# Seven block products for eight in half of an attention output projection, and smaller steps at the layer ends

## The chip, the cores and the metric

The kernel runs on one core of one Trainium2 chip. The metric is the device time in microseconds of one execution. The numbers below come from three timed runs and from one profiled execution of the kernel before.

## The reference

A decoder trunk of two layers works on 256 positions of width 2048, in float32. Layer 0 mixes by recurrences (RG-LRU and HGRN2), layer 1 by dilated attention with 16 heads of 128. Each is followed by an output projection, a residual sum, a norm and a squared-ReLU MLP of width 8192. What the change touches:

```python
out = (num / den).reshape(bsz, seq, D_MODEL).astype(h.dtype)   # the 16 heads, side by side
return out @ w_o                                               # 256 x 2048 by 2048 x 2048
...
h = h + mix
h = h + squared_relu_mlp(rms_norm(h, norm_mlp[layer]), w1[layer], w2[layer])
...
return rms_norm(h, final_norm)
```

## The kernel before

**Weights.** All weights come as units of 128 x 2048 numbers (1 MB). A unit is read into a `raw` tile (three buffers) and split in two: ACT casts the high part `hi` (`L104`), DVE subtracts to get the low part `lo` (`L105`), three buffers each. One float32 product is then three matmuls on PE: activation high by weight high, high by low, and low by high. `unit()` takes the next unit in a fixed list, `units`, and has the unit two places further fetched and split, with a raised priority (`stream`).

**Activations.** `bufa` holds the normed input of a projection, feature by feature, each feature block with its high and low half (512 numbers). `bufb` holds what goes into an output projection: block k of `bufb` is head k of the attention. `xres` (tile `xall` in the profile) is the residual, token by token: two halves j of 128 tokens, four column groups n of 512.

**A plain projection to tokens** (`tokens`, `out_project`): for a column group n, four units g (four feature blocks each) are multiplied for both token halves j, 2 x 4 x 3 = 24 matmuls of 512 columns a unit, into two banks of PSUM. `add_res` adds them to `xres`, and `to_features` transposes the four blocks back to `bufa` (two halves, each run from a list `turns` between units) and, for n < 2, forms the sums below.

**Seven products for eight** (`blocks`): for a pair of column groups and the first half of the features, the product is a 2 x 2 block product (token halves by even and odd feature blocks, even and odd rows of the weight by the two column groups) in the manner of Strassen and Winograd. Seven block products of twelve matmuls each replace eight: `a`, `t1`, `t2`, `c`, `t3`, `d`, `t4`. `t1`, `t2`, `t3` and `c` take sums of activation blocks, which `combos` and `part_forms` put into `formx` or `formh`. `t1`, `t2`, `t3` and `t4` take sums of weight units, which `combine` makes: tile `t` and tile `s`, by DVE (`L132`) or by an accumulating transfer on POOL's queue (`L144` to `L150`). The other half of the features goes through four plain units `n` (24 matmuls each). `ORDERS` fixes the sequence of the eleven units; the banks are `alpha`, `delta`, `gamma` (pool `p`) and `beta` (`pd`, `po` or `pt`). The MLPs (`first`, `second`) and the values of the attention already work so; the two output projections `w_out` and `w_o` are plain. In `second` a DVE sum makes the weight of `t4` (`s` plus `d`); in `first` and in the values a transfer does.

**What sets the order around the change.** A scheduler orders the instructions of every engine by priority and data; `mm` and `turn` chain the large products and the transposes of residuals on PE in the order of the program, whatever else is ready. The tiles of PSUM are allotted in the order of the program: whoever asks for `pd` or `po` waits until the earlier holder has been read.

**The attention's last heads.** For each head, `scores` makes q and k (two units), turns them (`rope`, on DVE), multiplies (`pl`), forms the softmax (DVE and ACT), transposes it (`pd`) and copies it (`pT`); `mix` multiplies it with the values (`po`) and splits the result into `bufb`. After head 15, `out_project(w_o, ...)` follows.

**Layer ends.** In the last quarter of an MLP, `done` follows each column group: `to_features` in layer 0; in layer 1, `xres` is multiplied by the final gain (`L799`).

Of the kernel before, what the change touches and what calls it, by code (L numbers as in the profile page):

```python
# [10 lines left out]
F32 = mybir.dt.float32  # L11
# [5 lines left out]
OP = mybir.AluOpType  # L17
# [3 lines left out]
P = 128  # L21
S = 256
# [19 lines left out]
def trunk_kernel(ctx, tc, x, xtok, cols, tab, masks, pos, fin, w_in, w_gate, w_out, w_qkv, w_o, w1, w2, out):  # L42
# [22 lines left out]
    units = []  # L65
    made = {}

    def plan(src, n):
        units.extend((src, i) for i in range(n))

    def plan2(src, i):
        for what, u in ORDERS[src is not w1]:
            units.append((src, None if u is None else i + u, what, i))

    where = {"x": (w_in, lambda i: i, 1), "y": (w_in, lambda i: 8 + i, 1), "g": (w_gate, lambda i: i, 1),
# [5 lines left out]
    for layer in range(2):  # L81
        if layer:
            for v, heads in ((0, 24), (32, 8)):
                plan2(w_qkv, v)
                units.extend((w_qkv, v + 8 + i) for i in range(heads))
            plan(w_o, 16)
        for q in range(4):
            for src in (w1, w2):
                for n in range(0, 4, 2):
                    plan2(src, layer * 64 + q * 16 + 4 * n)  # L90
# [35 lines left out]
    def combine(u, src, i, what, i0):  # L126
        def load(name, j, home=wraw):
            held[name] = home.tile([P, 2048], F32, name="raw" if home is wraw else name)
            nc.sync.dma_start(held[name], src[j])

        def add(to, x, y):
            V.tensor_tensor(held[to], held[x], held[y], OP.add)  # L132

        if what == "a":
            load("t1", i0 + 4, both)
            load("a", i)
            held["s"] = both.tile([P, 2048], F32, name="s")
            add("s", "a", "t1")
        elif what in ("n", "d"):
            load(what, i)  # L140
        ahead = units[u + 1][2:3] if u + 1 < len(units) else ()
        if ahead == ("t2",):
            load("c", i0 + 5)
            nc.gpsimd.dma_start(held["t1"], src[i0 + 5], accum_op=OP.add)  # L144
            add("s", "s", "c")
        if ahead == ("t4",) and src not in T4_DMA(w1, w2, w_qkv):
            add("s", "s", "d")
        made[u] = Weights(held[{"t1": "s", "t2": "s", "t3": "t1", "t4": "s"}.get(what, what)])
        if what == "c" and src in T4_DMA(w1, w2, w_qkv):
            nc.gpsimd.dma_start(held["s"], src[i0 + 1], accum_op=OP.add)  # L150

    def fetch_first():
# [178 lines left out]
            V.scalar_tensor_tensor(r, t, 1.5, r, op0=OP.add, op1=OP.mult)  # L331

    def tokens(src, i0, mov, kgs=(0, 1, 2, 3), by_k=False):
        ks = range(KB)
        ps = [pmm.tile([P, 512], F32, name="p") for _ in range(2)]
        for g in kgs:
            w = unit(src, i0 + g)
            order = [(j, i) for i in range(4) for j in range(2)] if by_k else \
                [(j, i) for j in range(2) for i in range(4)]
            for j, i in order:  # L340
                k = ks[4 * g + i]
                h, l = w.part(i * 512, 512)
                xh = mov[:, k, j * P:j * P + P]
                xl = mov[:, k, S + j * P:S + j * P + P]
                first, last = g == kgs[0] and i == 0, g == kgs[-1] and i == 3
                mm(ps[j], xh, h, start=first, stop=False)
                mm(ps[j], xh, l, start=False, stop=False)
                mm(ps[j], xl, h, start=False, stop=last)
            turn_some(1)
        return ps  # L350
# [268 lines left out]
    def to_features(n, gname, forms=None):  # L619
        def work(half):  # L620
            k = 4 * n + 2 * half
            with urgent():
                p = psc.tile([P, 2, S], F32, name="pl", bufs=2)
                for j in range(2):
                    for i in range(2):
                        turn(p[:, i, j * P:j * P + P], xres[:, j, (k + i) * P:(k + i) * P + P])
                if forms is None:
                    for i in range(2):
                        split_to(bufa[:, k + i], p[:, i], col(gname, k + i))
                    return  # L630
                z = pair.tile([P, 2, 2, P], F32, name="y4" if half else "y21")
                for i in range(2):
                    A.activation(z[:, i], p[:, i].rearrange("p (j c) -> p j c", j=2), AF.Copy, scale=col(gname, k + i))
                split_to(bufa[:, k:k + 2], z.rearrange("p i j c -> p i (j c)"))
                a11, a21, a12, a22 = (z[:, i, j] for i in range(2) for j in range(2))
                combos(a22, a11, a21, a12, a11, a21, a12, a22)
                part_forms(forms, k // 2, 1, slice(0, 4), z.rearrange("p i j (one c) -> p one (i j) c", one=1))
        turns.extend([0, lambda half=half: work(half)] for half in range(2))

    def out_project(src, gname, kgs):  # L640
        nrm = Norm()
        for n in range(4):
            add_res(tokens(src, 4 * n, bufb, kgs), n, nrm)
            to_features(n, gname, formx if n < 2 else None)
        return nrm
# [3 lines left out]
    def blocks(src, i0, n0, mov, forms, events, final):  # L649
# [4 lines left out]
                "c": lambda i: form(2, i)}  # L654
        alpha, delta, gamma = (pmm.tile([P, 512], F32, name="p") for _ in range(3))
        beta = psc.tile([P, 512], F32, name="pt" if src is w_qkv and i0 else "po" if n0 else "pd", bufs=1)
        bank = {"a": beta, "t1": alpha, "t2": beta, "c": alpha, "t3": beta, "d": gamma, "t4": beta}
        sums = {(0, 0): gamma, (0, 1): beta, (1, 0): alpha, (1, 1): delta}
        opened = []

# [6 lines left out]
                mm(bank, xh, l, start=False, stop=False, skip_group_check=True)  # L667
                mm(bank, xl, h, start=False, stop=i == 3, skip_group_check=True)

        plains = [0, 0]  # L670
        for what, u in ORDERS[src is not w1]:
            w = unit(src, None if u is None else i0 + 4 * n0 + u)
            due = len(later)
            if what != "n":
                times(bank[what], w, side[what])
                if what in events:
                    events[what](bank[what])
            else:
                n, g = divmod(u, 4)
                plains[n] += 1  # L680
                for j in (1, 0) if n else (0, 1):
                    times(sums[n, j], w, lambda i, j=j, g=g: plain(j, 4 * g + i))
                    if plains[n] == 2:
                        final(n, j, sums[n, j])
                flush(due)
            turn_some()
# [60 lines left out]
        blocks(w1, i0, n0, bufa, formx, {"a": hold("y1", A.copy, 2), "t1": hold("y4", V.tensor_copy), "t2": hold("y2", A.copy),  # L747
                                             "t3": u3}, final)

    def second(i0, n0, nrm, r2, r2n, done, gains):  # L750
        def to_x(bank, j, n, r, last):
            at = slice(n * 512, n * 512 + 512)
            with urgent():
                V.scalar_tensor_tensor(xres[:, j, at], bank, r[:, j:j + 1], xres[:, j, at], op0=OP.mult, op1=OP.add)  # L754
                if nrm and last:
                    nrm.add(j, n)

        def u2(bank):
            to_x(bank, 0, n0 + 1, r2n, False)
            if gains:  # L760
                gains()

        def u3(bank):
            to_x(bank, 1, n0 + 1, r2n, True)
            done(n0 + 1)

        blocks(w2, i0, n0, bufb, formh,
               {"a": lambda b: to_x(b, 0, n0, r2, False), "t1": lambda b: to_x(b, 1, n0 + 1, r2, False),
                "t2": u2, "t3": u3},
               lambda n, j, b: to_x(b, j, n0 + n, r2, (n, j) != (1, 1)))  # L770
        done(n0)

    def mlp(layer, nrm, nxt, gname):
# [13 lines left out]
        for q in range(4):  # L787
            ends = nxt if q == 3 else None

            def done(n):  # L790
                if ends is None:
                    return
                if gname:
                    to_features(n, gname, formx if n < 2 else None)
                elif n != LAST:
                    at = slice(n * 512, n * 512 + 512)
                    with urgent():
                        for j in range(2):
                            V.tensor_tensor(xres[:, j, at], xres[:, j, at], fing[n], OP.mult)  # L799

            for n in (0, 2):
                first(layer * 64 + q * 16, n)
# [129 lines left out]
    vg = values(32)  # L932
    for i, bank in enumerate((("po", 1), ("pd", 1), ("pl", 2), ("pl", 2))):
        mix(8 + i, pend[i], vg, *bank)
    for i in range(4):
        mix(12 + i, scores(40 + 2 * i), vg)

    mixers.close()
    pair, formh = open_pairs(1)
    nrm = out_project(w_o, "nmlp1", (0, 1, 2, 3))  # L940
    fnorm = Norm()
    fing = mlp(1, nrm, fnorm, None)
    done = [n for n in range(4) if n != LAST]
# [46 lines left out]
_A = (("a", 0), ("t1", 4))  # L990
_B = (("t2", 5), ("c", None))
_C = (("t3", None), ("d", 1), ("n", 2), ("t4", None), ("n", 3))
ORDERS = (_A + (("n", 6),) + _B + (("n", 7),) + _C, _A + (("n", 7),) + _B + (("n", 6),) + _C)
T4_DMA = lambda w1, w2, w_qkv: (w1, w_qkv)
NOSYNC = mybir.DependencyInfo(mybir.DependencyClass.NoSync, mybir.DependencyReason.DATA)


# [29 lines left out]
def _layout(a):  # L1027
# [25 lines left out]
    def gate(w):  # L1053
# [16 lines left out]
        "pos": c(n(a["positions"]).reshape(1, S)),  # L1070
        "fin": c(n(a["final_norm"]).reshape(1, D)),
        "w_in": c(np.concatenate(w_in)), "w_gate": c(w_gate), "w_out": c(toks(n(a["rec_w_out"][0]))),
        "w_qkv": c(np.concatenate(w_qkv)), "w_o": c(toks(n(a["attn_w_o"][0]))),
        "w1": w1, "w2": w2,
    }

# [17 lines left out]
```

## Time and profile before

| | us |
|---|---|
| three timed runs: median | 2164.65 |
| lowest, highest | 2163.99, 2165.69 |
| the profiled execution | 2164.17 |
| its span, first to last instruction | 2162.0 |
| PE busy in it | 2142.9 |
| DVE busy in it | 1819.7 |
| ACT busy in it | 1268.8 |

The profile shows one execution. Engines: PE multiplies (PEld loads its weights), DVE and ACT work on vectors, POOL and SP only issue transfers here. `L105` is line 105 of the kernel; in a group, `lo<-raw,hi` is the tile that is written and those that are read. A busy time counts each instruction from its start to its end; matmuls overlap, so their busy times add up to more than the time they take.

### The profile page before, as it was taken

What the parts mean: (1) busy time and instruction counts of PE and PEld (TensorE: products, weight loads), DVE (VectorE), ACT (ScalarE), POOL (GpSimd) and SP (SyncE); (2) the same over time, 40 slices, a digit from 0 to 9 for tenths busy, and PEclk for the clock granted to TensorE, in tenths of its full rate; (3) what the DMA queues carried; (4) which work ended last, traced back from release to release, by engine and by line L of the source; (5) the groups of instructions that cost most, each with busy time, mean ns of one, the idle gap of its engine ahead of it and who ended that gap; (6) DMA issues with size and microseconds to landing.
All of it is one profiled execution on the core that took longest, in us unless ns stands there. A gap on an engine that the chain in (4) does not pass through costs nothing.

```text
span 2162.0 us, 27706 instructions
## 1 busy us (share of the span) xinstructions
PE 2142.9 (99%) x11020; PEld 1829.1 (85%) x11020; DVE 1819.7 (84%) x2114; ACT 1268.8 (59%) x1415; POOL 48.0 (2%) x61
## 2 busy tenths in 40 slices
PE   9999999999999999999999999999999999999997
PEld 8999998888888888888788888888888888888886
DVE  7776787689889889889998897767998998998897
ACT  7444485566466566557665545455655755755764
POOL 0000000000000000000000000000000000000000
PEclk9999999999999999999999999999999999999999
DMA  8444446587777777787675556456868777777873
GB/s 319 157 156 162 152 155 214 178 243 246 229 237 250 233 238 243 237 251 226 209 249 197 173 163 227 157 190 218 246 219 254 238 229 246 241 234 228 261 238 129
DMA packets 66432, 468.86 MB, mean 217 GB/s; under 512 B 7408, under 2 KB 8176, under 8 KB 10368
## 3 DMA queue, kind: packets, MB, share of 16 engines
q1 hardware_dynamic: 58176, 410.89, 53.1%
q0 software_dynamic: 7840, 55.61, 13.8%
q8 instruction: 86, 1.41, 0.3%
q10 hardware_dynamic: 288, 0.61, 0.1%
q14 instruction: 42, 0.34, 0.0%
HBM read 464.98 MB, written 2.10 MB: 216 GB/s over the span
## 4 chain that ended last, share of the span: by engine, by line
PE 94%; DVE 3%; ACT 1%; DMA 1%; issue 1%; SPq 0%; DVEq 0%; ACTq 0%
PE p L183 65%; PE pd L183 12%; PE po L183 12%; PE pl L186 2%; DVE lo L105 1%; PE pl L479 1%; PE pt L183 1%; ACT hi L104 1%; DMA raw<-in_w 0%; DMA xall<-in_x 0%; PE pl L863 0%; PE po L884 0%; DVE xall L754 0%; PE pd L876 0%; PE pd L463 0%
## 5 line engine op out<-in xcount | busy, mean ns | idle before, releaser
L104 ACT CAST hi<-raw 128x2048 fp32r<-128x2048 f32 (+2 forms) x468 | 684.0, 1484 | 556.2 <-PE p L183 342.6
L105 DVE TENSOR_TENSOR lo<-raw,hi 128x2048 fp32r<-128x2048 f32 (+2 forms) x468 | 816.5, 1759 | 192.2 <-ACT hi L104 176.4
L183 PE MATMUL p<-hi,bufb 128*128 128x512 f32 x1408 | 450.1, 391 | 3.3 <-DVE xall L754 2.7
L183 PE MATMUL p<-hi,bufa 128*128 128x512 f32 x1136 | 365.8, 391 | 1.0 <-ACT hi L104 0.7
L183 PE MATMUL p<-bufa,hi 128*128 128x256 f32 (+1 forms) x1792 | 365.3, 317 | 0.1
L183 PEld LDWEIGHTS p<-hi,bufb 128*128 128x128 f32 x1408 | 264.1, 188 | 62.2 <-DVE xall L754 6.2
L183 PEld LDWEIGHTS p<-bufa,hi 128*128 128x128 f32 x1792 | 294.2, 190 | 18.6 <-DVE hz L421 0.3
L183 PE MATMUL p<-lo,bufb 128*128 128x512 f32 x704 | 274.4, 390 | 0.9 <-DVE lo L105 0.9
L183 PE MATMUL p<-bufa,lo 128*128 128x256 f32 x1152 | 256.6, 287 | 0.0
L183 PEld LDWEIGHTS p<-hi,bufa 128*128 128x128 f32 x1136 | 213.2, 188 | 48.3 <-DVE y L718 2.4
L105 DVE TENSOR_TENSOR lo<-s,hi 128x2048 fp32r<-128x2048 f32 x102 | 233.2, 2286 | 19.0 <-ACT hi L104 17.0
L104 ACT CAST hi<-s 128x2048 fp32r<-128x2048 f32 x102 | 195.2, 1914 | 52.9 <-PE po L183 22.4
L183 PE MATMUL p<-lo,bufa 128*128 128x512 f32 x568 | 221.9, 391 | 1.9 <-DVE lo L105 1.9
L183 PEld LDWEIGHTS p<-bufa,lo 128*128 128x128 f32 x1152 | 189.7, 191 | 2.7
L183 PEld LDWEIGHTS p<-lo,bufb 128*128 128x128 f32 x704 | 132.2, 188 | 28.0 <-DVE lo L105 1.2
L183 PEld LDWEIGHTS p<-lo,bufa 128*128 128x128 f32 x568 | 106.7, 188 | 25.5 <-DVE lo L105 4.1
L132 DVE TENSOR_TENSOR s<-s,raw 128x2048 f32<-128x2048 f32 x50 | 114.2, 2283 | 3.7 <-DMA raw<-in_w 3.7
L183 PE MATMUL pd<-hi,bufa 128*128 128x512 f32 x288 | 95.2, 392 | 0.0
L183 PE MATMUL p<-hi,formx 128*128 128x512 f32 x288 | 94.9, 390 | 0.0
L105 DVE TENSOR_TENSOR lo<-t,hi 128x2048 fp32r<-128x2048 f32 x34 | 77.8, 2288 | 13.0 <-ACT hi L104 13.0
L183 PE MATMUL po<-hi,bufa 128*128 128x512 f32 x256 | 84.8, 392 | 0.0
L183 PE MATMUL p<-hi,formh 128*128 128x512 f32 x256 | 84.0, 389 | 0.0
(302 smaller groups left out, 2875.8 us busy)
## 6 DMA issues: line engine op xcount, KB each, us to landing
raw<-in_w SPq DMA_DIRECT2D x224, 1024.0 KB, 5.0
raw<-in_w_in SPq DMA_DIRECT2D x46, 1024.0 KB, 4.9
raw<-in_w_qkv SPq DMA_DIRECT2D x46, 1024.0 KB, 4.9
t<-in_w SPq DMA_DIRECT2D x32, 1024.0 KB, 5.6
t<-in_w POOLq DMA_DIRECT2D x32, 1024.0 KB, 8.9
raw<-in_w_out SPq DMA_DIRECT2D x16, 1024.0 KB, 4.9
s<-in_w POOLq DMA_DIRECT2D x16, 1024.0 KB, 9.1
raw<-in_w_o SPq DMA_DIRECT2D x16, 1024.0 KB, 4.9
```

Of the source, the lines that this page charges most:

```text
L104: A.copy(h, w)
L105: V.tensor_tensor(l, w, h.bitcast(F32), OP.subtract)
L132: V.tensor_tensor(held[to], held[x], held[y], OP.add)
L183: chain[:] = [after(T.matmul(*args, **kw), chain)]
L186: chain[:] = [after(T.transpose(out_, in_, ident), chain)]
L479: T.matmul(pl[:, j], kq[:, js], halves(qp[:, js], c, True), start=True, stop=True)
```

## The change

It has five parts.

1. The first pair of column groups of `w_o` goes through `second`, with `src=w_o`, scale 1.0, and an order of its own: a plain unit first (`n`, 6), then `a`, `t1`, `n` 7, `t2`, `c`, `t3`, `d`, `n` 2, `t4`, `n` 3. `t1` gets a bank of its own (`po`), and unit 6 and 7 share `alpha` and `delta` from the start, so that one eviction (`e5`) serves two column groups and `final(1, 0)` comes after `c`. The second pair stays plain.
2. `mixed_forms` makes the sums of activations for it from heads 0 to 7 in `bufb`, in four steps by the last four heads.
3. The weight of `t4` is made by an accumulating transfer everywhere, in `second` too.
4. `to_features` with `forms` starts its second half one unit later than its first.
5. The gain products of column groups 0 and 1 at the end go through `turns`, some units later, without raised priority.

```diff
+    order_of = lambda src: ORDERS[0 if src is w1 else 2 if src is w_o else 1]
...
-            plan(w_o, 16)
+            plan2(w_o, 0)
+            units.extend((w_o, 8 + i) for i in range(8))
...
-        if ahead == ("t4",) and src not in T4_DMA(w1, w2, w_qkv):
-            add("s", "s", "d")
         made[u] = Weights(held[{"t1": "s", "t2": "s", "t3": "t1", "t4": "s"}.get(what, what)])
-        if what == "c" and src in T4_DMA(w1, w2, w_qkv):
+        if what == "c":
             nc.gpsimd.dma_start(held["s"], src[i0 + 1], accum_op=OP.add)
...
-        ks = range(KB)
+        ks = PAIRED if src is w_o else range(KB)
...
-        turns.extend([0, lambda half=half: work(half)] for half in range(2))
+        turns.extend([-half if forms else 0, lambda half=half: work(half)] for half in range(2))
-    def out_project(src, gname, kgs):
-        nrm = Norm()
-        for n in range(4):
+    def out_project(src, gname, kgs, ns=range(4), nrm=None):
+        nrm = nrm or Norm()
+        for n in ns:
...
-        bank = {"a": beta, "t1": alpha, "t2": beta, "c": alpha, "t3": beta, "d": gamma, "t4": beta}
+        bank = {"a": beta, "t1": psc.tile([P, 512], F32, name="po", bufs=1) if src is w_o else alpha, "t2": beta, "c": alpha, "t3": beta, "d": gamma, "t4": beta}
...
+                elif what == "c" and plains[1] == 2:
+                    final(1, 0, alpha)
...
-                    if plains[n] == 2:
+                    if plains[n] == 2 and (n, j, "c" in done) != (1, 0, False):
                         final(n, j, sums[n, j])
...
+        def e5(bank):
+            to_x(bank, 1, n0 + 1, r2, False)
+            if src is w_o:
+                to_x(bank, 0, n0 + 1, r2, False)
...
-                    at = slice(n * 512, n * 512 + 512)
-                    with urgent():
+                    def gain(n=n, at=slice(n * 512, n * 512 + 512)):
                         for j in range(2):
                             V.tensor_tensor(xres[:, j, at], xres[:, j, at], fing[n], OP.mult)
+                    if n < 2:
+                        turns.append([-3, gain])
+                    else:
+                        with urgent():
+                            gain()
...
+    z = both.tile([P, 2048], F32, name="s").rearrange("p (m i j c) -> p m i j c", m=4, i=2, j=2)
+
+    def mixed_forms(m):
+        zm, b = z[:, m], bufb[:, 2 * m:2 * m + 2].bitcast(F32)
+        V.tensor_tensor(zm.rearrange("p i j c -> p i (j c)"), b[..., :S], b[..., S:], OP.add)
+        a11, a21, a12, a22 = (zm[:, i, j] for i in range(2) for j in range(2))
+        combos(a22, a11, a21, a12, a11, a21, a12, a22)
+        part_forms(formx, m, 1, slice(0, 4), zm.rearrange("p i j (one c) -> p one (i j) c", one=1))
+
     for i in range(4):
         mix(12 + i, scores(40 + 2 * i), vg)
+        mixed_forms(i)
...
-    nrm = out_project(w_o, "nmlp1", (0, 1, 2, 3))
+    nrm = Norm()
+    second(0, 0, nrm, 1.0, -1.0, lambda n: to_features(n, "nmlp1", formx), src=w_o, forms=formx)
+    out_project(w_o, "nmlp1", (0, 1, 2, 3), (2, 3), nrm)
...
 _A = (("a", 0), ("t1", 4))
 _B = (("t2", 5), ("c", None))
 _C = (("t3", None), ("d", 1), ("n", 2), ("t4", None), ("n", 3))
-ORDERS = (_A + (("n", 6),) + _B + (("n", 7),) + _C, _A + (("n", 7),) + _B + (("n", 6),) + _C)
-T4_DMA = lambda w1, w2, w_qkv: (w1, w_qkv)
+ORDERS = (_A + (("n", 6),) + _B + (("n", 7),) + _C, _A + (("n", 7),) + _B + (("n", 6),) + _C,
+          (("n", 6),) + _A + (("n", 7),) + _B + _C)
```

The rows of `w_o` are laid out on the host in the paired order of feature blocks (0, 2, 4, 6, 1, 3, 5, 7, then 8 to 15), as those of the MLPs are; `ks = PAIRED` in `tokens` follows it.

More of the change, by code (lines that the diff above doesn't have):

```diff
@@ L66, in trunk_kernel @@
     made = {}
-    def plan(src, n):
-        units.extend((src, i) for i in range(n))
+    order_of = lambda src: ORDERS[0 if src is w1 else 2 if src is w_o else 1]
     def plan2(src, i):
-        for what, u in ORDERS[src is not w1]:
+        for what, u in order_of(src):
             units.append((src, None if u is None else i + u, what, i))
@@ L668, in times @@
                 mm(bank, xl, h, start=False, stop=i == 3, skip_group_check=True)
-        plains = [0, 0]
-        for what, u in ORDERS[src is not w1]:
+        plains, done = [0, 0], []
+        for what, u in order_of(src):
             w = unit(src, None if u is None else i0 + 4 * n0 + u)
             due = len(later)
+            done.append(what)
             if what != "n":
@@ L748, in first, with second @@
                                              "t3": u3}, final)
-    def second(i0, n0, nrm, r2, r2n, done, gains):
+    def second(i0, n0, nrm, r2, r2n, done, gains=None, src=w2, forms=None):
         def to_x(bank, j, n, r, last):
@@ L753, in to_x @@
             with urgent():
-                V.scalar_tensor_tensor(xres[:, j, at], bank, r[:, j:j + 1], xres[:, j, at], op0=OP.mult, op1=OP.add)
+                V.scalar_tensor_tensor(xres[:, j, at], bank, r if isinstance(r, float) else r[:, j:j + 1],
+                                       xres[:, j, at], op0=OP.mult, op1=OP.add)
                 if nrm and last:
                     nrm.add(j, n)
+        def e5(bank):
+            to_x(bank, 1, n0 + 1, r2, False)
+            if src is w_o:
+                to_x(bank, 0, n0 + 1, r2, False)
         def u2(bank):
@@ L765, in u3 @@
             done(n0 + 1)
-        blocks(w2, i0, n0, bufb, formh,
-               {"a": lambda b: to_x(b, 0, n0, r2, False), "t1": lambda b: to_x(b, 1, n0 + 1, r2, False),
-                "t2": u2, "t3": u3},
+        blocks(src, i0, n0, bufb, forms or formh,
+               {"a": lambda b: to_x(b, 0, n0, r2, False), "t1": e5, "t2": u2, "t3": u3},
                lambda n, j, b: to_x(b, j, n0 + n, r2, (n, j) != (1, 1)))
@@ L1072, in _layout @@
         "w_in": c(np.concatenate(w_in)), "w_gate": c(w_gate), "w_out": c(toks(n(a["rec_w_out"][0]))),
-        "w_qkv": c(np.concatenate(w_qkv)), "w_o": c(toks(n(a["attn_w_o"][0]))),
+        "w_qkv": c(np.concatenate(w_qkv)), "w_o": c(toks(n(a["attn_w_o"][0]), PAIRED)),
         "w1": w1, "w2": w2,
```

## Prediction

> **What bounds the kernel now.** I read the page first (span, busy shares, clock), then who waited for whom on PE, then the chain of waits around the projection, then the timelines of DVE and ACT there, then busy times by stage.
>
> ```profile
> span 2162.0 us, 27706 instructions
> PE 2142.9 (99%) x11020; PEld 1829.1 (85%) x11020; DVE 1819.7 (84%) x2114; ACT 1268.8 (59%) x1415; POOL 48.0 (2%) x61
> ```
> ```profile
> PE p L183 <- DVE lo L105: 2.8, 5, 0.9
> PE p L183 <- DVE xall L754: 2.7, 2, 1.4
> ```
> TensorE is the bound, nearly without a hole: all waits of PE together are under 10 us. So a removed matmul is worth its whole spacing, and a hole in PE costs its whole length.
>
> ```profile
> 1394.13 0.11 PE pd L876
> ...
> 1396.32 0.22 PE pl L862 x2
> 1396.54 0.43 PE pl L863 x2
> 1396.97 2.52 PE p L183 x11
> 1399.49 0.43 PE po L884 x2
> ...
> 1403.82 0.11 PE pd L876
> ...
> 1407.15 0.43 PE po L884 x2
> 1407.59 0.24 PE po L885 x2
> ...
> 1408.27 9.46 PE p L183 x39
> 1417.72 0.87 PE pl L186 x8
> 1418.60 21.78 PE p L183 x96
> ```
> This chain is in order of time. Two things are to be seen. First, 96 matmuls take 21.78 us: one costs 0.227 us of PE, not the 391 ns of its own row, since they overlap. Second, the attention of heads 14 and 15 (scores `pl`, transposes of the weights `pd`, mix `po`) lies between products of `w_o` (`p L183`): heads 0 to 11 are enough for three of the first column group's four units, so PE has about 90 products to do while DVE and ACT make the last softmaxes. The stage runs from 1386.5 to 1434.9 (end of column group 1; 1418.60 plus 72 x 0.227): **48.4 us**.
>
> **The change, part by part.** Building the changed program gives the order of instructions on each engine; every time below is from the trace of before.
>
> *The products.* Fifteen block products of twelve matmuls stand for sixteen: 12 x 0.227 = **-2.7 us**. No other matmul goes.
>
> *What covers the softmax.* This decides. The new order starts with unit n6 (24 products, 5.4 us), and then `a` writes bank `pd` and `t1` bank `po`, the banks that heads 14 and 15 still need. The order on PE is therefore: 24 products; `pd` of 14; `po` of 14; `pl` of 15; `pd` of 15; `po` of 15; `a`. Between them stands no product at all. The durations:
>
> ```profile
> 1397.01 0.56 DVE L865 SCALAR_TENSOR_TENSOR as<-pl,tab__181 128x384 f32<-128x384 f32 x1 [1.43 <-PE pl L863]
> 1397.60 0.61 DVE L869 TENSOR_REDUCE nm<-as 128x1 f32<-128x128 f32 x2
> 1398.94 0.17 DVE L871 RECIPROCAL ll<-ll 128x2 f32<-128x2 f32 x1 [0.73 <-ACT as L214]
> 1399.14 0.55 DVE L873 TENSOR_SCALAR as<-as,ll 128x128 f32<-128x128 f32 x2
> ```
> ```profile
> 1398.93 1.28 ACT L214 ACT_TABLE_LOAD   x1
> 1400.22 0.20 ACT L214 ACTIVATE spare<-epsc 128x1 f32<-128x1 f32 x1
> ```
> From the scores' first matmul (1396.15 in PE's timeline) to the end of the scaling (1399.69) are 3.55 us; the transposes take 0.33, the copy of `pT` ends 0.8 after the last one starts (1394.42 to 1395.21), the mix takes 0.65. I step through the new order:
> - The products of `w_o` start at 1386.5 as before; n6 ends at 1391.9.
> - `pl` of 14 now stands behind 15 of the 16 `lo` matmuls of its neighbour, at 1385.15 for 1383.4. Its first softmax half on DVE ends at 1387.2 (0.86 + 1.2 after it). Behind it on DVE stand the split of `t1` (2.29), a mix's low part (0.42), `hz` (0.4), the sum `s<-s,raw` for `t2` (2.28), `hz` (0.42), and only then the scaling (0.55): 1393.4. PE idles 1.5 us; the transposes end at 1393.8.
> - Copy of `pT`, mix of 14: 1394.5 to 1395.2.
> - Head 15's rotation on DVE follows that scaling (shuffle and two products 1.0), then the split of n7 (2.29), then its last sum (0.41): 1397.0. `pl` of 15 starts at 1397.1.
> - Softmax of 15: 3.55, to 1400.65; its transposes; ACT is in the table load until 1401.35, so `pT` is ready at 1401.9 and the mix ends at **1402.6**, where `a` starts.
>
> So 10.7 us lie between n6 and `a`, with 2.6 us of matmuls in them. After it: thirteen times 2.72 (seven block products and three plain units, each plain one two) = 35.4, eight transposes 0.9: 1438.9. Against 1434.9: **+4.0 us**, the saved 2.7 already in it. I followed DVE and ACT beyond `a` too: splits there end 0.3 to 5 us ahead of their products, so I add nothing. Bounds: with no queue on DVE the stretch is 0.3 + 0.8 + 0.65 + 3.55 + 0.3 + 1.0 + 0.65 = 7.3, hence +0.6; with one more split (2.29) in front +6.3.
>
> *TensorE's clock.* PE has had no such hole before, so the trace shows only its end:
>
> ```profile
> 2148.00:2152.00 4.00, 4.00 (x19) 3.13 (x17) 1.31 (x5) 0.93 (x3) 0.00 (x0) 1.00 0.00 0
> 2152.00:2154.90 2.90, 0.18 (x1) 0.00 (x0) 2.53 (x8) 1.84 (x5) 0.00 (x0) 1.00 0.00 0
> 2154.90:2162.00 7.10, 0.00 (x0) 0.00 (x0) 1.47 (x4) 1.54 (x3) 0.00 (x0) 0.50 0.74 295
> ```
> The granted clock (third number from the end) goes to 0.50 at 2154.9, 2.7 us after the last matmul (2152.18). At the start the first matmuls are 0.213 us apart until 4.5 us, then 0.111: the clock was half for 3.45 us of work. The hole above has 2.6 us of matmuls in 10.7 us, and one stretch of 2.7 us with none. I take it that the clock drops, and costs half of 3.45 us: **+1.7 us**. Bounds: 0, and 3.4 for two such periods. [...]
>
> *The new forms* (`mixed_forms`). DVE 4 x 0.69 + 16 x 0.20 + 4 x 0.69 = 8.7 us, ACT 4 x 0.62, placed at the second half of `values(32)` and head 12. Between 1323 and 1346 DVE is idle for about 9 us and PE's next units are split 3 to 6 us ahead: 0. Without that cover, up to +2.
>
> *`s` by DMA* in the pairs of `second`. Sixteen sums of 2.28 us leave DVE, sixteen accumulating transfers join POOL's queue.
>
> ```profile
> L132 DVE TENSOR_TENSOR s<-s,raw 128x2048 f32<-128x2048 f32 x50 | 114.2, 2283 | 3.7 <-DMA raw<-in_w 3.7
> ```
> ```profile
> s<-in_w POOLq DMA_DIRECT2D x16, 1024.0 KB, 9.1
> ```
> Nothing on PE waits for those sums: both waits of PE for `xall` (1066 and 2118) hang on a chain that begins at a split which ACT's cast released, the cast by PE's freeing of the buffer, after that sum. The transfer has 9.1 us, and products of some 24 us between `t2`'s split and `t4`. The pairs of `first` already work so, at a DMA share of 0.82 for 0.71, without waits of PE. POOL has nothing else to do. 0; bounds -2.7 (all waits for `xall` go) and +2 (raw loads late).
>
> *Layer ends.* Where eight transposes stood together, twice four stand now, at six places. A group costs about 0.09 us beside its transposes (timeline): +0.5. At the end of layer 0 a 0.6 us low part of `formx` and 0.3 us of combinations move out of the queue ahead of the eviction that PE waits for, while four transposes come behind it: -0.4. At the end of layer 1 the order on DVE between `t1`'s split and that eviction is the same, and its gain product (0.68) is still ahead of it: the wait of 1.5 us stays. The final part is unchanged.
>
> **Sum.** The profiled execution took 2164.17 us (span 2162.0 and 2.2 around it), 0.5 under the median of the three runs, 2164.65, and within their spread. 2164.17 + 4.0 + 1.7 + 0.5 - 0.4 = **2170.0 us**, 0.25% slower than the median. A measurement of this kernel can tell about 0.2% (4.3 us) from no change.
>
> **Rivals.**
> - *The clock holds.* The five small groups of matmuls in the hole count as enough. For it: no stretch without any is longer than the 2.7 us after which the trace shows the drop. 2164.17 + 4.0 + 0.1 = 2168.3: within 0.2%.
> - *The softmax stays covered, and the layer ends lose their waits.* Faster: if PE reached `a` without waiting for heads 14 and 15, the stage would save the 2.7 us; with the two waits for `xall` (2.7 us) gone through the lighter DVE queue, 2164.17 - 5.4 = 2158.8. It takes that the hole costs under about 1 us. Against it: the chain for head 15 alone, scores to mix, is 5.5 us and nothing stands beside it.
> - *A longer hole.* The raw block of `t2`'s sum comes late (one load near 1047.7 takes 9.6 us, not 5), which stops DVE ahead of the scaling of 14, and the clock stays half for two periods: 2164.17 + 6.3 + 3.4 + 0.1 = 2174.
> - *The hole at its floor, full clock*: 2164.17 + 0.6 + 0.1 = 2164.9.
>
> **Chances.** Forecast 0.52, clock holds 0.27, longer hole 0.10, floor 0.06, faster 0.05. Of the forecast's share nearly a fifth, by a somewhat shorter hole, falls under 2169.0; of the rival's with full clock a fourth above it. Slower by over 0.2%: 0.59 with the longer hole; rounded 0.62, since I found more that can be late than early. Within: 0.33. Faster: 0.05. The range leaves out the floor, the faster case and the outer half of the longer hole: 2166.5 to 2173.5.
>
> **What would show it.** Right: PE has some 8 us of waits between the 24 products of n6 and `a`, for DVE `as` L883 (before: L873), DVE `hz` and ACT `pT`; granted clock under 1.00 there and in the next few us; matmuls 0.43 apart for about 3.4 us; stage 53 to 55 us for 48.4. Wrong: products of `w_o` between `pd` of 14 and `po` of 15; a stage under 48 us; waits for a raw block or for POOL's transfers in the pairs of `second`.

## The result and the profile after

The changed kernel takes **2170.09 us** (median of ten runs, 2169.61 to 2171.09), the kernel before 2164.78 (ten runs, 2163.99 to 2165.69): ratio 1.0026, 95% interval 1.0017 to 1.0034. It is slower. The profiled execution of the changed kernel took 2170.47 us; its page begins:

```profile
span 2168.7 us, 27753 instructions
...
PE 2144.1 (99%) x11008; PEld 1829.9 (84%) x11008; DVE 1807.1 (83%) x2124; ACT 1276.2 (59%) x1414; POOL 63.6 (3%) x79
```

Twelve matmuls fewer, as intended, and a span that is 6.7 us longer. That page hints at the place only by one 8 among the nines of PE's busy tenths, in the slice from about 1355 to 1410 us. The time between the first product of `w_o` and the first product of the MLP after it says it (starts in PE's timeline; the first two lines are of the kernel before, the others of the changed one):

```profile
1386.46 0.40 PE L183 MATMUL p<-hi,bufb 128*128 128x512 f32 x1
1480.09 0.39 PE L183 MATMUL pd<-hi,bufa 128*128 128x512 f32 x1
...
1386.55 0.40 PE L181 MATMUL p<-hi,bufb 128*128 128x512 f32 x1
1486.83 0.39 PE L181 MATMUL pd<-hi,bufa 128*128 128x512 f32 x1
```

That is 93.63 us before and **100.28 us** after, +6.65 of the 6.7: what lies outside the projection adds up to the same within 0.1 us. Between the medians lie only 5.3 us: the profiled run of before was 0.6 us under its median and that of after 0.4 over, and an execution takes some time outside its span, 2.2 us before and 1.8 after.

Who waited for whom on PE (in total, times, longest):

```profile
PE pd L886 <- DVE as L883: 3.5, 2, 2.7
PE p L181 <- DVE lo L105: 2.8, 4, 1.0
PE p L181 <- DVE xall L755: 2.2, 2, 1.4
PE po L894 <- ACT pT L888: 1.5, 2, 0.9
PE pl L872 <- DVE hz L862: 1.4, 1, 1.4
```

The second and third lines stood in the profile before. The first, fourth and fifth are new, 6.4 us, and name the softmax of heads 14 and 15: its scaling, its copy, and the turned `k`. The chain of waits there, start and length of each piece:

```profile
1386.59 5.60 PE p L181 x25
...
1392.21 1.91 ACT hi L104
...
1394.15 2.29 DVE lo L105
1396.44 0.33 DVE hz L862
...
1396.82 0.79 PE pl L872 x2
...
1402.57 1.22 PE po L894 x2
...
1404.22 3.79 PE pd L181 x12
1408.01 2.72 PE po L181 x12
```

Unit n 6 ends at 1392.2; `a` (the twelve matmuls into `pd`) starts at 1404.2. Twelve microseconds, the hole, lie between them with not one product of `w_o`. Before, this stretch was filled: `PE p L183 x11` between `pl` and `po`, and so on. Two more things are to be seen. The chain passes through a weight's split (`hi`, then `lo`, 4.2 us) that has nothing to do with the softmax: n 6's end frees a buffer, ACT casts n 7 into it, and DVE's split of n 7 stands ahead of the last sum of head 15's rotation. And `a` takes 3.79 us, where `t1` behind it, with as many matmuls, takes 2.72. The reason is in the busy times by stage (the third number from the end is the granted clock):

```profile
1380.00:1396.08 16.08, 13.71 (x72) 11.14 (x70) 14.48 (x25) 6.56 (x11) 0.00 (x0) 1.00 0.34 121
1396.08:1406.32 10.24, 6.27 (x17) 4.50 (x18) 3.33 (x10) 3.32 (x8) 0.00 (x0) 0.50 0.29 102
1406.32:1441.60 35.28, 35.28 (x161) 29.21 (x160) 28.86 (x29) 22.37 (x24) 0.86 (x1) 1.00 0.64 209
```

The clock is halved for 10.24 us. In the kernel before it is full throughout this stage:

```profile
1386.50:1434.90 48.40, 47.94 (x221) 39.28 (x220) 30.22 (x49) 24.06 (x41) 0.00 (x0) 1.00 0.47 155
```

### The profile page after: what moved, and what is told of

Same layout as the page of the kernel before. It is cut to its first block, busy times and chain, and to the rows that moved or that the text cites. A ratio compares the mean times of both kernels' runs of the same rounds, so it can differ in the third digit from the quotient of the medians.

```text
span 2168.7 us, 27753 instructions
## 1 busy us (share of the span) xinstructions
PE 2144.1 (99%) x11008; PEld 1829.9 (84%) x11008; DVE 1807.1 (83%) x2124; ACT 1276.2 (59%) x1414; POOL 63.6 (3%) x79
## 4 chain that ended last, share of the span: by engine, by line
PE 94%; DVE 3%; ACT 1%; issue 1%; DMA 1%; SPq 0%; DVEq 0%; ACTq 0%
PE p L181 64%; PE pd L181 13%; PE po L181 12%; PE pl L184 2%; DVE lo L105 1%; PE pl L477 1%; PE pt L181 1%; ACT hi L104 1%; DMA raw<-in_w 0%; PE pl L873 0%; PE po L894 0%; DMA xall<-in_x 0%; DVE xall L755 0%; PE pd L886 0%; PE pl L872 0%
## 5 line engine op out<-in xcount | busy, mean ns | idle before, releaser
L181 PE MATMUL p<-hi,bufb 128*128 128x512 f32 x1336 | 428.3, 391 | 2.4 <-DVE xall L755 2.2
L181 PEld LDWEIGHTS p<-hi,bufb 128*128 128x128 f32 x1336 | 250.8, 188 | 57.5 <-DVE xall L755 5.8
L181 PE MATMUL p<-lo,bufb 128*128 128x512 f32 x668 | 260.2, 389 | 1.0 <-DVE lo L105 1.0
L105 DVE TENSOR_TENSOR lo<-s,hi 128x2048 fp32r<-128x2048 f32 x105 | 240.0, 2286 | 19.9 <-ACT hi L104 17.8
L104 ACT CAST hi<-s 128x2048 fp32r<-128x2048 f32 x105 | 200.8, 1913 | 55.5 <-PE po L181 21.3
L181 PEld LDWEIGHTS p<-lo,bufb 128*128 128x128 f32 x668 | 125.5, 188 | 26.8 <-DVE lo L105 1.3
L181 PE MATMUL pd<-hi,bufb 128*128 128x512 f32 x288 | 94.5, 393 | 0.0
```

What stands on the lines that cost most here:

```text
L104: A.copy(h, w)
L105: V.tensor_tensor(l, w, h.bitcast(F32), OP.subtract)
L181: chain[:] = [after(T.matmul(*args, **kw), chain)]
```

## Theories and experiments

**A** (the prediction's): the banks `pd` and `po` leave the softmaxes of heads 14 and 15 bare, the halved clock adds to it, and the rest of the change costs about nothing. **B**: the loss comes from the other parts (sixteen added transfers, layer ends). **C**: the clock is only a companion of the hole and costs nothing. **E, F**: seven products for eight bring waits of their own wherever they stand, since DVE has sums of weights to make. Each run has its own runs of the kernel before beside it, 2164.2 to 2164.5 us.

**e1: the projection plain again, the rest of the change kept.**

```diff
-            plan2(w_o, 0)
-            units.extend((w_o, 8 + i) for i in range(8))
+            units.extend((w_o, i) for i in range(16))
...
-    nrm = Norm()
-    second(0, 0, nrm, 1.0, -1.0, lambda n: to_features(n, "nmlp1", formx), src=w_o, forms=formx)
-    out_project(w_o, "nmlp1", (0, 1, 2, 3), (2, 3), nrm)
+    nrm = out_project(w_o, "nmlp1", (0, 1, 2, 3))
```

> The first pair of column groups of w_o is plain again (sixteen block products); the other parts of the change stay (weights of t4 by accumulating transfers in the MLPs, second half of the transposes one unit later, gain products later). Theory A (the loss is the bare softmax of heads 14 and 15 in the projection's stage, 6.6 us): the stage goes back to 48.4 us and the time to 2163.5 to 2164.8 us, at or a little under the kernel before. Rival B (the loss comes from the sixteen added transfers or from the layer ends): 2167 us or more, and the stage is not shorter than in the changed kernel by 6 us. Granted clock 1.00 in the stage under A.

Measured 2163.65 us; ratio to before 0.9997 (0.9988 to 1.0006). From the first product of `w_o` to the first of the MLP: 93.72 us. B falls: the other parts are worth nothing that can be told from zero.

**e2: the projection alone.**

```diff
+        if ahead == ("t4",) and src is w2:
+            add("s", "s", "d")
-        if what == "c":
+        if what == "c" and src is not w2:
...
-        turns.extend([-half if forms else 0, lambda half=half: work(half)] for half in range(2))
+        turns.extend([0, lambda half=half: work(half)] for half in range(2))
```

(and the gain products as before.)

> Only the projection's pair goes by seven block products; in the MLPs the weight of t4 is made on DVE again, and the second half of the transposes and the gain products stand as before. Theory A: the whole loss is here, stage about 55 us, time 2169.5 to 2171 us, at or a few tenths above the changed kernel. Rival B: within 1 us of the kernel before, 2164 to 2166 us.

Measured 2170.56 us, ratio 1.0029 (1.0018 to 1.0039); the projection takes 100.36 us. The whole loss is here.

**e3: the hole filled.** Products of a constant by itself keep TensorE busy, and the transposes of the softmax come behind them; the order of work on DVE and ACT is that of the changed kernel.

```diff
+    def fillers(count, last):
+        idle = psc.tile([P, P], F32, name="pt", bufs=1)
+        for _ in range(count):
+            last[:] = [after(T.matmul(idle, ones, ones, start=True, stop=True), last)]
...
+        if hd == 14:
+            idle_mm[:] = [after(m, [])]
+            fillers(6, idle_mm)
...
+        if fill:
+            fillers(fill, last)
...
-        mix(12 + i, scores(40 + 2 * i), vg)
+        mix(12 + i, scores(40 + 2 * i, 14 if i == 3 else 0), vg)
```

> The changed kernel with twenty 128x128 products of a constant by itself (result not used) put on TensorE in the hole: six after the mix of head 14, fourteen after the scores of head 15. DVE and ACT have the same chain as in the changed kernel, so the hole keeps its length where the clock is full. Theory A (the granted clock falls to 0.50 because TensorE is too little used in the hole, and that costs about 2.7 us): clock 1.00 through the stage, products of `a` 0.227 us apart from the first, stage 55.0 to about 52.3 us, time about 2167.4 (2166.6 to 2168.4). Rival C (the slow clock costs nothing, since everything in the hole waits for DVE and ACT): 2170 to 2172. Rival D (the clock falls whatever TensorE does): clock 0.50 there again, 2170 or more.

Measured 2167.78 us (2166.91 to 2169.61), 2.3 under the changed kernel. Its chain of waits and its busy times by stage:

```profile
1394.43 1.34 PE pt L869 x12
...
1401.65 2.75 PE pd L181 x12
```
```profile
1391.20:1401.60 10.40, 8.12 (x59) 7.27 (x60) 6.70 (x17) 5.56 (x10) 0.00 (x0) 1.00 0.30 101
```

With twenty products more in it the hole is *shorter*: 10.5 us (1391.2 to 1401.65) for 12.0, `a` takes 2.75 for 3.79, and the projection 97.68 for 100.28. So a halved clock costs not only the products that follow: the small matmuls of the softmax, which stand one behind the other with waits between them, are stretched as well (`pl` 0.94 us here, 1.66 there; `po` 0.92 and 1.65). C and D fall. Of the eleven runs, the three with a mean clock of 0.997 took 2168.9 to 2169.6, most others 2166.9 to 2168.1. The trace is of one of the fastest, so it is likely, but not shown, that the filled hole doesn't hold the clock every time.

**e10: only the later part filled.** As e3 without `fillers(6, idle_mm)`.

> Run e3 without the six products of a constant before the scores of head 15; the fourteen behind those scores stay (results not used). In the changed kernel the clock fell at 1396.1, at the end of a window of 3.41 us in which TensorE had only about 1.0 us of small matmuls; the hole's later windows are filled here. Theory A (a window too little used halves the clock in the windows that follow it, until a used one ends): the clock falls at the same place, near 1396, and is full again after one or two windows of 3.41 us in place of three; time between e3 and the changed kernel, 2168 to 2169.5. Rival J (the clock falls only when several windows are too little used): clock 1.00 through the stage, 2167.4 to 2168.

Measured 2169.74 us (2168.79 to 2171.82). Chain and stage:

```profile
1398.51 4.02 PE pt L877 x28
```
```profile
1396.84:1400.25 3.41, 3.39 (x14) 3.21 (x15) 1.47 (x4) 0.73 (x3) 0.00 (x0) 0.50 0.80 269
```

The clock fell at 1396.84, within 0.8 us of the place in the changed kernel, and was full again 3.41 us later (at 1400.25), where the changed kernel took 10.24: J falls, and the clock did as A expected. The time is a miss at the upper end: the first fillers ran at half clock, 28 matmuls in 4.02 us in place of 3.1 (estimated from e3, twelve in 1.34), and held back the transposes (`pd` at 1402.5) that they were to serve. The run tells of the clock, not of what it costs.

**e6: `a` freed from the bank.**

```diff
-name="pt" if src is w_qkv and i0 else "po" if n0 else "pd", bufs=1)
+name="pt" if src is w_o or src is w_qkv and i0 else "po" if n0 else "pd", bufs=1)
```

> The changed kernel with one edit: `a` gets the bank `pt` in place of `pd`, so its twelve products (2.7 us) needn't wait for the transposes of heads 14 and 15 and follow n 6 at once; t1 keeps `po` and still waits. Theory A (the end of the hole is set by DVE and ACT, so products moved into it are a clean gain): 2.7 us less than the changed kernel with the clock halved as before, 2167.4; if the shorter hole also keeps the clock full, 2165. So 2164.5 to 2168. Rival G (the chain of the softmax moves back with the products, since the splits hang on their ends): 2169.5 to 2171.

Measured 2170.18 us, as the changed kernel: A's expectation failed, and the time is G's. The profiled execution took 2171.94, the longest of the six. DVE's timeline and, last, a line of the chain:

```profile
1396.95 0.67 DVE L755 SCALAR_TENSOR_TENSOR xall<-pt,xall 128x512 f32<-128x512 f32 x1
1397.55 2.27 DVE L105 TENSOR_TENSOR lo<-s,hi 128x2048 fp32r<-128x2048 f32 x1
1399.75 0.54 DVE L875 SCALAR_TENSOR_TENSOR as<-pl,tab__181 128x384 f32<-128x384 f32 x1
...
1406.51 5.49 PE po L181 x12
```

`a` ran at once behind n 6, in the hole's first 2.7 us. That let its eviction (`xall<-pt`) and the split of `t1`'s weight start, 2.9 us together, while the scores of head 15 were still being made (1397.1 to 1398.0), and head 15's softmax (`as`) had to wait for their end. So G's chain did move back, but by less than `a` had gained: the mix of head 15 ends 13.2 us after n 6, in the changed kernel 12.0. The rest was lost behind it. `t1` now waits 0.9 us until DVE has read the low part of head 15 out of its bank, a wait that `a` had covered, and its twelve products run at half clock from the first to the last, 5.49 us for 2.72 (granted clock 0.50 from 1406.50 to 1412.00).

**e7: the sum for `t2` by a transfer.**

```diff
-            add("s", "s", "c")
+            if src is w_o:
+                nc.gpsimd.dma_start(held["s"], src[i0 + 5], accum_op=OP.add)
+            else:
+                add("s", "s", "c")
```

> The changed kernel, but for w_o the sum of weights for t2 (2.28 us of DVE, which stands ahead of the scaling of head 14) is made by an accumulating transfer on POOL's queue. Theory A with DVE's queue as the prediction stepped through it: the scaling of 14 is done before n 6 ends, so the 2.7 us wait for `as` goes, the scores of head 15 come about 4 us earlier (1392.3 in place of 1396.8), behind them one split (2.29), and `a` starts near 1400 to 1401.5 in place of 1404.2: 2166 to 2168 us. Rival H (the sum isn't what holds the softmax: the split of n 7, which waits for the end of n 6, holds it anyway): 2169.5 to 2171. Rival I (the transfer is late for t2): a wait of TensorE for a low part in t2, 2170 or more.

Measured 2167.60 us (2166.89 to 2168.37); the projection takes 97.61 us. From its chain:

```profile
1392.19 1.91 ACT hi L104
...
1394.12 2.29 DVE lo L105
...
1401.44 3.86 PE pd L184 x12
```

`a` starts at 1401.44, 2.8 us earlier. So DVE's queue set the hole's length, as the prediction's steps had it: one sum of 2.28 us less stands in front of the scaling of 14. H's time and I fall. But the split that H names is in the chain still: it now stands on DVE inside head 15's softmax, ahead of the reduction (`nm`), and the hole, 9.3 us here, begins with its cast.

**e4 and e8: no block product waits for a bank of the softmax.** Both have `beta` in `pt` and `t1` in `alpha`, with the eviction `e5` as in the MLPs; e4's order is the one below, e8's is that of the first matrix of the MLPs. In e4 unit n 7 comes after `t3`, so the norm and the transposes of column group 1 are taken without n 7's products.

```diff
-          (("n", 6),) + _A + (("n", 7),) + _B + _C)
+          _A + (("n", 6),) + _B + (("t3", None), ("d", 1), ("n", 2), ("n", 7), ("t4", None), ("n", 3)))
```

> The changed kernel with `beta` in the bank `pt` and `t1` in `alpha`, so that no block product waits for the banks of heads 14 and 15, and with the order a, t1, n 6, t2, c, t3, d, n 2, n 7, t4, n 3. Products of w_o then stand between the scores, transposes and mixes of heads 14 and 15. Theory A (the seven products are worth their 2.7 us and only the cover was lost): no wait of TensorE over 1 us in the stage, clock 1.00, stage 45.7 to 47 us, time 2161 to 2163 us, under the kernel before. Rival E (the queue of DVE with the sums of weights is what holds the stage, whatever the banks): waits for `as` or for low parts of weights remain, stage 48 us or more, time 2165 or more.

> The changed kernel with `a` in bank `pt` and t1 in `alpha`, and the order a, t1, n 6, t2, c, n 7, t3, d, n 2, t4, n 3, so that no block product waits for the banks of heads 14 and 15. In run e4 the sums and splits of weights got ahead of the last softmax on DVE and ACT, and a stall of about 10 us came later, in place of the hole. Theory A (only the banks matter): 2161 to 2163. Theory E (with seven products the splits come faster than DVE and ACT can make them beside two softmaxes, so the hole moves): a stall of several us between the scores of head 15 and n 7, time 2165 to 2168.

Measured 2166.68 us (e4) and 2167.52 us (e8). A fails in both, and the times are E's. With the banks free, TensorE runs ahead, its finished units release the next splits, and these stand ahead of the softmaxes and inside them. In e4, DVE at the softmax of head 15 (`as` was released by the scores, which ended at 1409.0):

```profile
1408.08 2.27 DVE L105 TENSOR_TENSOR lo<-raw,hi 128x2048 fp32r<-128x2048 f32 x1
1410.28 0.54 DVE L873 SCALAR_TENSOR_TENSOR as<-pl,tab__181 128x384 f32<-128x384 f32 x1
1410.75 2.27 DVE L105 TENSOR_TENSOR lo<-s,hi 128x2048 fp32r<-128x2048 f32 x1
1412.94 0.59 DVE L877 TENSOR_REDUCE nm<-as 128x1 f32<-128x128 f32 x2
```

The hole is smaller and comes later. In e4 it is 1418.6 to 1423.9, 5.3 us with one product of `w_o` in them; PE waits there 1.8 and 1.5 us for the halves of the mixes (`bufb`), not for `as` or low parts of weights, which E had named, and the clock is halved for about 7 us (0.56 on average from 1419.90 to 1423.30, and the 15 matmuls from 1423.94 on take 5.16 us). In e8 it is 1404.2 to 1413.4, 9.2 us with three products. So freeing the banks wins some 3 us of the changed kernel's 5.3 back, and not the 8 that A counted on. No run changed the priority of the splits, so that it alone decides is not shown.

**e5: the other pair.** The first pair of column groups is plain (its products cover the softmax, as before the change) and the second goes by seven block products, when no softmax is left.

```diff
-            plan2(w_o, 0)
-            units.extend((w_o, 8 + i) for i in range(8))
+            units.extend((w_o, i) for i in range(8))
+            plan2(w_o, 8)
...
-        part_forms(formx, m, 1, slice(0, 4), zm.rearrange("p i j (one c) -> p one (i j) c", one=1))
+        part_forms(formh, m, 1, slice(0, 4), zm.rearrange("p i j (one c) -> p one (i j) c", one=1))
...
+    turns.extend([-i, lambda i=i: mixed_forms(i)] for i in range(4))
+    nrm = out_project(w_o, "nmlp1", (0, 1, 2, 3), (0, 1))
+    second(0, 2, nrm, 1.0, -1.0, lambda n: to_features(n, "nmlp1"), src=w_o, forms=formh)
```

> The other way round: the first pair of column groups of w_o plain, the second pair by seven block products in the order of the MLPs' second matrix, with the sums of heads 0 to 7 made in formh during the first pair. The softmaxes of heads 14 and 15 then have the plain products beside them, as in the kernel before. Theory A (the seven products are worth 2.7 us wherever the softmax is covered): no wait of TensorE over 1 us around heads 14 and 15, clock 1.00, and 2.7 us less than with the plain projection (2163.65): 2161.0 us (2160.3 to 2162.0). Rival F (seven products bring waits of their own, by sums of weights on DVE or transfers on POOL's queue, wherever they stand): 2163 or more, with waits of TensorE for low parts of weights in the second pair.

Measured 2167.46 us: A's number failed. Yet the projection takes 91.17 us, 2.46 under before. The loss comes behind it, in the first units of the MLP:

```profile
1481.00 2.45 PE p L181 x11
...
1483.47 2.29 DVE lo L105
...
1486.43 2.19 DVE lo L105
1488.63 0.41 DVE bufa L243
...
1489.59 6.72 PE p L181 x21
```

Column group 2 is now finished last, and the MLP's third unit (n 6) needs its features, while two splits stand ahead of them on DVE: 5.6 us of hole, and then 21 matmuls in 6.72 us (0.32 each for 0.227), with the clock at half for some 3.4 us (0.51 on average from 1490.30 to 1493.70).

**e9: e5 with n 7 ahead of n 6 in that one MLP quarter.**

```diff
-    order_of = lambda src: ORDERS[0 if src is w1 else 1]
+    order_of = lambda src, i: ORDERS[0 if src is w1 and i // 16 != 4 else 1]
```

> Run e5 with one edit: the first product of layer 1's first MLP quarter takes its units in the order a, t1, n 7, t2, c, n 6 in place of a, t1, n 6, t2, c, n 7. In e5 the projection itself gave its 2.7 us, but its second pair ends with column groups 2 and 3 close together, column group 2 last, and unit n 6, third in the MLP, needs the features of group 2: TensorE waited 5.6 us (1483.5 to 1489.1) and its clock was halved for 3.4 us. Theory A (that end was the whole loss of e5): no wait over 1.5 us there, clock 1.00, 2160.5 to 2162 us, under both kernels. Rival F (the seven products of the second pair have waits of their own): 2164 us or more.

Measured **2161.01 us** (2160.51 to 2161.95), ratio to before 0.9985 (0.9976 to 0.9994), under both kernels. The same place in its chain:

```profile
1480.45 2.72 PE p L181 x12
1483.17 0.87 PE pl L184 x8
1484.05 5.46 PE p L181 x24
```

No wait. Against e1, which has the plain projection and not the swap of n 6 and n 7, it is 2.64 us; the projection alone is 91.17 us for 93.72, 2.55 less; twelve matmuls of 0.227 are 2.72. F falls.

## Why the prediction came true

- *The sum, 2170.0.* It is within 0.1 us of the median, and part of that is luck. It starts from the profiled 2164.17, which is 0.6 under the median of the ten runs of before, and adds 5.8, which is 0.5 more than the medians' 5.3; the two errors cancel. The stage took 55.06 us (1386.55 to 1441.61), at the upper end of the 53 to 55 expected.
- *The products, -2.7.* Right, and shown where nothing covers it up: 2.64 by the times in e9, 2.55 by its projection.
- *What covers the softmax, +4.0.* Right in place and size. The order of DVE was as stepped through: transposes of 14 at 1393.0 (predicted 1393.4), their copy done at 1394.5 (1394.5), scores of 15 at 1396.8 (1397.1). At full clock the hole is 10.5 us (e3), predicted 10.7. With the clock's 2.60 us (projection of after less that of e3) taken out, the projection is 4.05 us longer than before, the saved 2.7 in it. That DVE's queue makes the hole is shown by e7; e6 shows DVE's delay too, but lost its gain in part otherwise.
- *TensorE's clock, +1.7.* Right in kind, too small: 2.6 us by the two traces, 2.3 by the medians, within the stated bounds of 0 and 3.4. The step that was mis-sized: "the clock drops, and costs half of 3.45 us", one period. It was half for 10.24 us, three times as long; of its three thirds only the last has matmuls throughout (3.41 us, 1.65 and 1.21 in the others). `a` lost 1.0 in it, and `pl` and `po` of head 15, which the sum had at full clock, 0.7 each. The hole therefore ended at 1404.2, not 1402.6, and the waits in it came to 6.4 us, not 8: the matmuls in it fill more of it, since they stand alone (transposes of 14 take 0.61 us and its mix 0.92, at full clock, where the sum had 0.33 and 0.65) and those of 15 are slowed as well.
- *`mixed_forms`, 0; `s` by a transfer, 0.* Right. The first product of `w_o` starts at 1386.55 for 1386.46, and the time outside the projection is the same within 0.1 us; no wait for POOL's transfers is in the list.
- *Layer ends, +0.5 and -0.4.* The -0.4 is seen: set against before, PE's products are 0.4 us late ahead of the end of layer 0 (1028.30 for 1027.87) and level behind it (1090.73 for 1090.67). Another 0.4 us is won in the last quarter of layer 1's MLP (6.74 us late behind the projection, 6.38 from 2097 on), where nothing was forecast; the +0.5 for smaller groups of transposes isn't seen. The profiled run's start-up is 0.3 to 0.4 us later and so is its end behind the last product, so the sum is nil, and e1 against before, -0.5, can't be told from zero. The waits for `xall` stay, 2.2 us for 2.7.
- *The rivals.* That the clock holds (0.27) failed at the figure by which it was argued: no stretch of the hole without a matmul is longer than 2.7 us, and the clock fell nevertheless. The longer hole would have been 2174, and the floor 2164.9; neither happened. The faster case failed at the chain of head 15, as held against it.

The stretches at half clock are 10.24 us long in the changed kernel (1396.08 to 1406.32), 6.83 in e7 (1396.85 to 1403.68) and 3.41 in e10 (1396.84 to 1400.25): three, two and one times 3.413. The clock's two falls in the changed kernel, at 1396.08 and at 2160.67, are 764.59 us apart, 224 times 3.413. Why it changes in such steps, and how little use makes it fall, the runs do not show.

## What to carry to other kernels

When work is removed from the engine that bounds, look at what that work was covering: here 2.7 us of products saved laid bare a softmax chain of 12 us, and the same saving moved 48 us later, to where nothing leans on it, was worth its full price. Freeing a bank or a buffer does not by itself cover a serial chain (e4, e6, e8): the engine that runs ahead releases prefetched work for the others, and where that work gets into their queues first, the chain moves back. Before counting on a stage's gain, look at what its last results feed: e5 and e9 differ by one swap of two units, and by 6.45 us.

## What was not expected of the hardware

In the 3.41 us ahead of the clock's fall in the changed kernel (1392.67 to 1396.08) matmuls were busy for 1.53 us, by the busy times by stage. Of the three thirds of its stretch at half clock the first two have 1.65 and 1.21 us, and the last, after which the clock was full, 3.41; the whole stretch of e10 has 3.39. Two stretches of that length in other runs: the first line is of e6, where half clock followed; the second of e5, where it didn't:

```profile
12.71:16.13 3.42, 1.89 (x7) 1.20 (x7) 3.33 (x11) 3.42 (x7) 0.00 (x0) 1.00 1.05 433
1483.43:1486.85 3.42, 1.75 (x12) 1.13 (x10) 3.38 (x4) 3.15 (x6) 0.79 (x1) 1.00 0.77 263
```

Busy time as the profile has it gives no sharp limit: 1.89 us in the one, 1.75 in the other. In the changed kernel's hole, where small matmuls alternate with waits, the clock was at 0.50 for 10.24 us, and twenty useless products made the kernel 2.3 us faster. The stretch at half clock in e6, some 16 us after the start, is one that before and after don't have: the mean clock of its profiled run is 0.995, that of after's 0.996, and its first products of `w_o` stand in the chain 0.25 us later (1386.84 for 1386.59). In the kernel before, 11.35 to 14.76 has 1.93 us and was followed by full clock. The work there is the same; what makes the difference is not shown.
